# Cross-attention projections in wide token-stationary blocks, some of them with seven products

## The chip, the cores and the metric

The kernel runs on one core of one Trainium2 chip. The metric is the time on the device in microseconds (us), the median of several executions. The core has five engines that this text speaks of: PE (TensorE, matrix products), DVE (VectorE), ACT (ScalarE), POOL (GpSimd, nearly idle here) and SP (SyncE, which only issues the transfers). Each takes its own instructions in a fixed order; between engines they wait for each other by semaphores.

## What is computed

One layer of an encoder on 256 tokens of 2048 channels, all in f32: a half-step SwiGLU FFN, a mixer (pooling and gated linear attention), a cross-attention to 256 memory tokens, a second FFN, and a last RMSNorm. The change touches the cross-attention alone:

```python
def mem_cross_attention(h, mem_h, w_q, w_kv, w_o):
    q = (h @ w_q).reshape(b, s, XATTN_HEADS, XATTN_HEAD_DIM)          # 4 heads of 512
    kv = (mem_h @ w_kv).reshape(b, mem_h.shape[1], 2, XATTN_HEADS, XATTN_HEAD_DIM)
    k, v = kv[:, :, 0], kv[:, :, 1]
    logits = jnp.einsum('bshd,bmhd->bhsm', q, k).astype(jnp.float32) * (XATTN_HEAD_DIM ** -0.5)
    p = jax.nn.softmax(logits, axis=-1).astype(v.dtype)
    o = jnp.einsum('bhsm,bmhd->bshd', p, v).reshape(b, s, D_MODEL)
    return o @ w_o
...
        x = x + mem_cross_attention(rms_norm(x, xattn_norm[l]), rms_norm(mem, mem_norm[l]),
                                    xattn_w_q[l], xattn_w_kv[l], xattn_w_o[l])
```

h and mem_h have 256 rows and 2048 columns; w_q is 2048 x 2048 and w_kv 2048 x 4096.

## The kernel before

**Numbers in two parts.** PE multiplies fp32r values, which hold fewer bits than f32. Each operand is therefore split into a high part (ACT copies it to fp32r) and a low part (DVE subtracts the high part from the source). A product is made of three: high x high, high x low, low x high. Weights go through the same split on their way: a transfer brings 1 MB into `raw`, ACT writes `wh`, DVE writes `wl` (lines 261 and 262).

**Units.** All weights are read as units of 1 MB, numbered through the program; unit 182 is the first of w_q, 198 the first of w_kv, 230 the first of w_o. The class `Stream` emits them: a unit's split is emitted two units ahead of its products (AHEAD = 2), three `raw` buffers are on their way (RAW = 3), and `wh` and `wl` have three buffers, so the split of unit u waits until PE is done with unit u - 3. Other work is put in with `st.op(f, n)`: it is emitted after n further units. The framework then orders each engine's instructions, so what is emitted late can stand earlier or later on an engine.

**Three block forms.** `block_a` (line 307) is feature-stationary: weights are the stationary operand, 512 columns at a time, and the result has features in rows. Per 128 rows of weight and 128 columns it takes one product with a moving operand of 512 (both parts of the activations) and one of 256; a unit has 32 products. `block_t` and `block_b` are token-stationary: a tile of 128 tokens is the stationary operand, and 512 columns of weights stream; a unit has 24 products, and tokens are in rows. `block_s` (line 469) is token-stationary with 1024 columns at a time, so a unit is two chunks of 128 rows x 1024 columns (a pair). Some of its pairs, the sevens, replace the eight block products of a 2 x 2 scheme by seven (as Strassen and Winograd do): 21 products instead of 24. For these, sums of the activations are made once (`Sums.make`, tile `ye`), and per unit sums of the weights in a tile `T` (line 442), which are split like weights (`split_seven`: `xh`, `xl` for three of the raw quarters, `wh`, `wl` for T). PSUM has four tiles of [128, 2, 512]. A `block_s` with sevens holds all four: two for the whole results and two for parts; `combine` adds the parts up after the last seven and frees two, `join` adds them to the whole after the last unit.

**The cross-attention before.** Four `block_a` for the queries, one head each, so q comes out with features in rows, as the logits want it; `ev_Q` joins the halves and multiplies by the row factor R of the norm, which `spread_norm` had spread over the partitions. Then, head by head: `block_a` for the keys, `logits`, `probs`, `block_b` for the values, `values`. The activations of both come from the same tile `xs`: `fold` (line 727) transposes x into it (tiles `px`, 16 per half of x), and `mem_fold` (line 1201, tiles `tm`) later puts the memory tokens in its place. Both write high parts on ACT (line 230) and low parts on DVE (line 231). `mem_fold(c)` writes chunks 4c to 4c + 3, and was emitted after units 2, 3, 4 and 5 of the last head's stretch, one group at a time between units.

The lines that the steps touch:

```python
    for h in range(H):
        if h == H - 1:
            for c in range(4):
                st.op(lambda c=c: mem_fold(c), c + 2)
        block_a(wblock(w_q, h * NB), xs, ev_Q(h))
```

## Time and profile before

| | |
|---|---|
| median of 3 runs | 2093.89 us (2093.42 to 2094.82) |
| profiled execution | 2093.61 us |
| its span | 2091.2 us |
| PE busy | 2079.7 us, 99% |
| DVE busy | 1729.1 us, 83% |
| ACT busy | 1115.5 us, 53% |
| granted TensorE clock | 0.998 |

The profiled execution's own time is 2.4 us above its span, which runs from the first to the last instruction; it is 0.3 us below the median. Busy time is the union of an engine's instructions, but matmuls overlap in their pipeline: a single one is shown with about 390 ns where the next starts about 227 ns later. What a stretch of products costs is therefore read from starts or from the chain, not from the mean of one.

### The profile page before, as it was taken

Reading aid. Unit: us, or ns where it says so; the run is one execution under the profiler, and the core shown is the slowest. Engines: PE = TensorE matmul, PEld = TensorE weight load, DVE = VectorE, ACT = ScalarE, POOL = GpSimd, SP = SyncE. Lnnn points to the kernel's source line nnn. Section 1 sums busy time; section 2 is a strip of 40 time slices with the busy share of each in tenths; the row PEclk is TensorE's granted clock in tenths of the full one; section 3 lists DMA queues with packets and bytes.
Section 4 is the critical chain, followed back from the end, with each engine's and each line's share of the span. In section 5 each row is a group of like instructions: output and inputs, shape, how many; then the busy total and the mean of one; then the engine's idle time right before and its main releaser. Section 6 shows DMA issues by size and latency. Waiting matters only on the chain.

```text
span 2091.2 us, 24553 instructions
## 1 busy us (share of the span) xinstructions
PE 2079.7 (99%) x9901; PEld 1741.6 (83%) x9901; DVE 1729.1 (83%) x1568; ACT 1115.5 (53%) x1096; POOL 14.2 (1%) x41
## 2 busy tenths in 40 slices
PE   9999999999999999999999999999999999999998
PEld 7888888888888888888888888888888888888886
DVE  7999899989998677688665555879998999989974
ACT  7655455645554555365645444556554556545544
POOL 0000000000000000000000000000000000000001
PEclk9999999999999999999999999999999999999999
DMA  7656666567656655468655555656576765676673
GB/s 263 203 200 231 231 221 218 185 224 245 216 199 241 215 179 195 151 193 269 233 181 170 170 165 167 228 190 220 181 241 211 244 203 187 223 241 221 207 257 119
DMA packets 143608, 435.94 MB, mean 208 GB/s; under 512 B 9860, under 2 KB 13544, under 8 KB 143112
## 3 DMA queue, kind: packets, MB, share of 16 engines
q1 hardware_dynamic: 143464, 434.38, 62.7%
q8 instruction: 77, 1.26, 0.2%
q14 instruction: 35, 0.29, 0.0%
q10 hardware_dynamic: 32, 0.01, 0.0%
HBM read 417.58 MB, written 16.78 MB: 208 GB/s over the span
## 4 chain that ended last, share of the span: by engine, by line
PE 96%; DVE 2%; issue 1%; ACT 0%; DMA 0%; SPq 0%; DVEq 0%
PE pt L344 45%; PE pt L465 22%; PE pa L329 15%; PE pb L344 6%; PE pe L344 3%; PE ph L821 1%; PE pl L1247 1%; PE pv L1284 1%; PE px L733 1%; DVE wl L446 0%; DVE T L442 0%; DVE wl L262 0%; DVE xl L262 0%; PE pp L958 0%; DMA x<-in_x 0%
## 5 line engine op out<-in xcount | busy, mean ns | idle before, releaser
L262 DVE TENSOR_TENSOR wl<-raw,wh 128x2048 fp32r<-128x2048 f32 (+2 forms) x279 | 626.4, 2250 | 231.3 <-ACT wh L261 230.3
L261 ACT CAST wh<-raw 128x2048 fp32r<-128x2048 f32 (+2 forms) x279 | 523.2, 1880 | 336.4 <-PE pt L344 106.6
L344 PE MATMUL pt<-wh,xs 128*128 128x512 f32 x1536 | 495.0, 390 | 0.2 <-ACT xs L230 0.2
L344 PE MATMUL pt<-wh,ys 128*128 128x512 f32 x1360 | 427.7, 390 | 0.0
L445 ACT CAST wh<-T 128x1024 fp32r<-128x1024 f32 x206 | 217.0, 1054 | 347.0 <-DVE T L442 336.4
L344 PEld LDWEIGHTS pt<-wh,xs 128*128 128x128 f32 x1536 | 287.6, 188 | 59.3 <-ACT xs L230 0.4
L329 PE MATMUL pa<-xs,wh 128*128 128x512 f32 x896 | 316.0, 397 | 0.0
L344 PE MATMUL pt<-wl,xs 128*128 128x512 f32 x768 | 299.8, 390 | 0.0
L344 PEld LDWEIGHTS pt<-wh,ys 128*128 128x128 f32 x1360 | 254.9, 188 | 52.6
L344 PE MATMUL pt<-wl,ys 128*128 128x512 f32 x680 | 264.9, 390 | 0.0
L329 PE MATMUL pa<-xs,wl 128*128 128x256 f32 x896 | 248.4, 281 | 0.0
L446 DVE TENSOR_TENSOR wl<-T,wh 128x2048 fp32r<-128x2048 f32 x103 | 235.3, 2284 | 1.3 <-ACT wh L445 1.3
L329 PEld LDWEIGHTS pa<-xs,wh 128*128 128x128 f32 x896 | 167.6, 188 | 38.1 <-issue 0.3
L262 DVE TENSOR_TENSOR xl<-raw,xh 128x1536 fp32r<-128x1536 f32 x103 | 180.4, 1751 | 0.0
L329 PEld LDWEIGHTS pa<-xs,wl 128*128 128x128 f32 x896 | 169.1, 189 | 1.7 <-issue 0.2
L344 PEld LDWEIGHTS pt<-wl,xs 128*128 128x128 f32 x768 | 144.2, 188 | 30.0 <-DVE wl L262 0.2
L261 ACT CAST xh<-raw 128x1536 fp32r<-128x1536 f32 x103 | 152.4, 1479 | 13.4 <-DMA raw<-in_ffn_w_gate 8.7
L344 PEld LDWEIGHTS pt<-wl,ys 128*128 128x128 f32 x680 | 127.7, 188 | 26.3
L442 DVE TENSOR_TENSOR T<-T,raw 128x512 f32<-128x512 f32 x206 | 142.3, 691 | 5.7
L442 DVE TENSOR_TENSOR T<-raw 128x1024 f32<-128x1024 f32 x103 | 125.5, 1219 | 0.5
L465 PE MATMUL pt<-wh,xs 128*128 128x512 f32 x320 | 124.5, 389 | 0.0
L465 PE MATMUL pt<-wh,xe 128*128 128x512 f32 x320 | 124.5, 389 | 0.0
(236 smaller groups left out, 2412.1 us busy)
## 6 DMA issues: line engine op xcount, KB each, us to landing
raw<-in_ffn_w_down SPq DMA_DIRECT2D x88, 1024.0 KB, 5.6
raw<-in_ffn_w_up SPq DMA_DIRECT2D x80, 1024.0 KB, 5.1
raw<-in_ffn_w_gate SPq DMA_DIRECT2D x77, 1024.0 KB, 5.1
raw<-in_w_in SPq DMA_DIRECT2D x32, 1024.0 KB, 5.2
raw<-in_xattn_w_kv SPq DMA_DIRECT2D x32, 1024.0 KB, 5.4
raw<-in_w_out SPq DMA_DIRECT2D x16, 1024.0 KB, 5.6
raw<-in_xattn_w_q SPq DMA_DIRECT2D x16, 1024.0 KB, 5.5
raw<-in_xattn_w_o SPq DMA_DIRECT2D x16, 1024.0 KB, 5.7
```

The costliest lines, as they stand in the source:

```text
L261: in_turn("scalar", lambda: nc.scalar.copy(hi, src))
L262: in_turn("vector", lambda: nc.vector.tensor_tensor(out=lo, in0=src, in1=f32(hi), op=ALU.subtract))
L329: nc.tensor.matmul(o, w, x, start=k == 0 and i == 0, stop=last and i == 1)
L344: nc.tensor.matmul(ps, a, w, start=first and i == 0, stop=last and i == 2)
L442: in_turn("vector", lambda: nc.vector.tensor_tensor(out=o, in0=a, in1=b, op=ALU.add))
L445: in_turn("scalar", lambda: nc.scalar.copy(th[:, c], t[:, c]))
L446: in_turn("vector", lambda: nc.vector.tensor_tensor(out=tl, in0=t, in1=f32(th), op=ALU.subtract))
L465: nc.tensor.matmul(banks[n], x, w, start=n in fresh and j == 0, stop=n in ends and j == 2)
L733: nc.tensor.transpose(v[:, j, h * P : (h + 1) * P], x[:, h, j * P : (j + 1) * P], ident)
L821: nc.tensor.transpose(v[:, i, h * P : (h + 1) * P], g[:, h, i * P : (i + 1) * P], ident)
L1247: nc.tensor.matmul(ps[:, t, :M], ys[:, 4 * h + d, a, tok], xa["K"][:, d, b, :], start=i == 0, stop=i == 11,)
L1284: nc.tensor.matmul(ps[:, d, :S], xa["V"][:, m, a, col], xa["PT"][:, m, b, :], start=i == 0, stop=i == 5,)
```

## The change

Queries, keys and values are now made by `block_s`, two heads (1024 columns) at a time: two blocks for w_q with pairs 1, 2 and 3 as sevens, two for the keys and two for the values with pairs 0 and 2 as sevens. That makes 6 + 4 + 4 = 14 sevens among 48 units. The order in which a block takes its pairs is written out (`Q_ORDER`, `KV_ORDER`). Q and K now come with tokens in rows; `rows_turned` transposes them, 8 transposes of 128 x 128 for each head (`turn_Q`, `turn_K`). The row factor of Q is a per-row scale on ACT, and R is no longer spread. Logits, softmax and values keep their work, for two heads one after the other. `mem_fold` is emitted after units 7, 7, 8 and 8 counted from the end of the first query block. The weight sums `T` use the buffers of `sg` (x rows and block results), and `xh`, `xl` share two buffers `att`; which tiles share is switched between the stretches (`homes`).

```diff
 
+    def rows_turned(g):
+
+        v = four(ptile(uid("ph")))
+        for i in range(4):
+            for h in range(2):
+                nc.tensor.transpose(
+                    v[:, i, h * P : (h + 1) * P], g[:, h, i * P : (i + 1) * P], ident
+                )
+        return v
...
-    st.op(open_scope("s_x", {
-        "T": [("kv", D, 2)], "xh": [("kv", D, 2), ("att", 3 * NB, 3)], "xl": [("att", 3 * NB, 3)],
-        "t": [("att", 3 * NB, 3)], "P": [("att", 3 * NB, 3)],
-        "PT": [("att", 3 * NB, 3)],
-    }), 1)
+
+    OUT_HOMES = {"T": [("kv", D, 2)], "xh": [("kv", D, 2), ("att", 3 * NB, 2)],
+                 "xl": [("att", 3 * NB, 2), ("PT", D, 1)]}
+    Q_HOMES = {"T": [("sg", D, 2)], "xh": [("att", 3 * NB, 2)],
+               "xl": [("PT", D, 1), ("att", 3 * NB, 2)]}
+    KV_HOMES = {"T": [("sg", D, 2)], "xh": [("att", 3 * NB, 2)], "xl": [("att", 3 * NB, 2)]}
+
+    def homes(of):
+        return lambda: scope.update(shared={tag: list(of[tag]) for tag in of})
+
+    st.op(open_scope("s_x"), 1)
+    st.op(homes(OUT_HOMES), 1)
...
-    into_x(I["w_out"][0], ys, 1.0, G_X)
+    into_x(I["w_out"][0], ys, 1.0, G_X, spread_too=False)
+    st.op(homes(Q_HOMES))
     st.op(mem_in, 2)
...
-    def ev_Q(h):
-        def evict(p, ps):
-            t = ttile()
-            joined(ps, t, rows["R"])
-            split_pair(ys, 4 * h + 2 * p, t)
+
+    q_sums, Q_ORDER = Sums("ye", xs, (1, 2, 3), True, 2), ((0, 6, 1, 4, 2, 5, 3, 7),
+                                                           (0, 4, 1, 5, 2, 6, 3, 7))
+    kv_sums, KV_ORDER = Sums("ye", xs, (0, 2), True, 2), (1, 3, 4, 0, 5, 6, 2, 7)
+    held = {}
+
+    def ev_Q(b):
+        def evict(j, c):
+            for h in range(2):
+                nc.scalar.activation(c[:, h, :], c[:, h, :], AF.Copy, scale=Rcol[:, h : h + 1])
+            held["Q", b, j] = c
         return evict
 
-    def ev_K(p, ps):
-        if p == 0:
-            xt("K", [P, 4, 2, M], F32R, tag="kv", bufs=2)
-        t = ttile()
-        joined(ps, t)
-        split_pair(xa["K"], 2 * p, t)
-
-    def ev_V(ps):
-        V = xt("V", [P, 2, 2, XHD], F32R, tag="kv", bufs=2)
-        split(V[:, :, 0, :], V[:, :, 1, :], ps)
+    def turn_Q(b, j):
+        k = 8 * b + 4 * j
+        split(ys[:, k : k + 4, 0, :], ys[:, k : k + 4, 1, :], rows_turned(held["Q", b, j]))
+
+    def turn_K(h):
+        v = rows_turned(held["K", h])
+        K = xa["K", h] = xt("K", [P, 4, 2, M], F32R, tag="kv", bufs=2)
+        split(K[:, :, 0, :], K[:, :, 1, :], v)
+
+    def ev_V(b):
+        def evict(j, c):
+            V = xa["V", 2 * b + j] = xt("V", [P, 2, 2, XHD], F32R, tag="kv", bufs=2)
+            split(V[:, :, 0, :], V[:, :, 1, :], c)
+        return evict
...
-        nm, sm = xt("nm", [P, 2]), xt("sm", [P, 2])
+        nm, sm = xt("nm", [P, 2], bufs=2), xt("sm", [P, 2], bufs=2)
...
-        pr = xa["P"] = shared_tile("P", 2 * M, F32, uid("P"), 1).rearrange("p (t m) -> p t m", t=2)
+        pr = xa["P", h] = xt("P", [P, 2, M], bufs=2)
...
-        PT = xa["PT"] = shared_tile("PT", 4 * S, F32R, uid("PT"), 1).rearrange(
+        if h % 2 == 0:
+            xt("PT", [P, D], F32R)
+        PT = xa["PT", h] = xa["PT"][:, h % 2 * 4 * S : (h % 2 + 1) * 4 * S].rearrange(
             "p (m a s) -> p m a s", m=2, a=2
         )
...
-    for h in range(H):
-        if h == H - 1:
-            for c in range(4):
-                st.op(lambda c=c: mem_fold(c), c + 2)
-        block_a(wblock(w_q, h * NB), xs, ev_Q(h))
-    for h in range(H):
-        block_a(wblock(w_kv, h * NB), xs, ev_K)
-        st.op(lambda h=h: logits(h), 2)
-        st.op(lambda h=h: probs(h), 3)
-        block_b(wblock(w_kv, D + h * NB), xs, ev_V)
-        st.op(lambda h=h: values(h), 1)
+    for g, after in zip(q_sums.pairs, (0, 1, 3)):
+        st.op(lambda g=g: among_weights(lambda: q_sums.make(g)), after)
+    for b in range(2):
+        block_s(wwide(w_q, b * 2 * NB), xs, q_sums, Q_ORDER[b], ev_Q(b))
+        for j in (1, 0):
+            st.op(lambda b=b, j=j: turn_Q(b, j), 1)
+        if b == 0:
+            for c, after in enumerate((7, 7, 8, 8)):
+                st.op(lambda c=c: mem_fold(c), after)
+    st.op(homes(KV_HOMES))
+    for g, after in zip(kv_sums.pairs, (1, 2)):
+        st.op(lambda g=g: among_weights(lambda: kv_sums.make(g)), after)
+    for b in range(2):
+        block_s(wwide(w_kv, b * 2 * NB), xs, kv_sums, KV_ORDER, lambda j, c, b=b: held.__setitem__(
+            ("K", 2 * b + j), c))
+        for j in (1, 0):
+            h = 2 * b + j
+            st.op(lambda h=h: turn_K(h), 1)
+        for h in (2 * b, 2 * b + 1):
+            st.op(lambda h=h: logits(h), 2)
+            st.op(lambda h=h: probs(h), 3)
+        block_s(wwide(w_kv, D + b * 2 * NB), xs, kv_sums, KV_ORDER, ev_V(b))
+        for h in (2 * b, 2 * b + 1):
+            st.op(lambda h=h: values(h), 1)
+    st.op(homes(OUT_HOMES))
     OUTPUT.make_sums()
     into_x(w_o, ys, 1.0, G_FFN2, spread_too=False)
     st.op(close_scope, 1)
```

How it moves instructions is shown at two places.

The first place is the start of the queries, on DVE. Tiles: `x267` holds the second half of x, and the two lines that write it from `pt259` and `pt260` add the last results of w_out; `px` are its transposes, of which the low parts go to `xs`; `wl184` belongs to the third unit of w_q. Before:

```order
L710 SCALAR_TENSOR_TENSOR x267_7136<-pt259_7038,x267_7136 128x2x512
L710 SCALAR_TENSOR_TENSOR x267_7136<-pt260_7039,x267_7136 128x2x512
L262 TENSOR_TENSOR wl184_7336<-raw184_7245,wh184_7335 128x2048
L283 TENSOR_REDUCE sums_101<-ss_100 128x2
L206 TENSOR_SCALAR chain_102<-sums_101 128x2
L210 RECIPROCAL Rcol_98<-chain_102 128x2
L216 TENSOR_TENSOR chain_102<-chain_102,Rcol_98 128x2
L217 TENSOR_TENSOR chain_102<-chain_102 128x2
L218 RECIPROCAL Rcol_98<-chain_102 128x2
L222 TENSOR_SCALAR diag279_7462<-ident_73,Rcol_98 128x128
L231 SCALAR_TENSOR_TENSOR xs_107<-px273_7375,gains_97,xs_107 128x256
```

Now, from just before the second of these additions on:

```order
L413 TENSOR_TENSOR j272_7336<-j272_7336 128x128
L713 SCALAR_TENSOR_TENSOR x267_7136<-pt260_7039,x267_7136 128x2x512
L414 TENSOR_TENSOR j272_7336<-j272_7336 128x128
L268 TENSOR_TENSOR xs_107<-j272_7336,xs_107 128x128
L415 SCALAR_TENSOR_TENSOR j272_7336<-j272_7336 128x128
L418 TENSOR_TENSOR j272_7336<-j272_7336 128x128
L445 TENSOR_TENSOR T184_7346<-raw184_7245 128x1024
L268 TENSOR_TENSOR ye271_7335<-j272_7336,ye271_7335 128x384
L445 TENSOR_TENSOR T184_7346<-T184_7346,raw184_7245 128x512 x2
L262 TENSOR_TENSOR xl184_7350<-raw184_7245,xh184_7349 128x1536
L449 TENSOR_TENSOR wl184_7348<-T184_7346,wh184_7347 128x2048
L231 SCALAR_TENSOR_TENSOR xs_107<-px275_7387,gains_97,xs_107 128x256
```

Unit 184 was a plain unit of one DVE instruction; it is a seven now, and its sums and both its low parts, with the sums of the activations (`j272`, `ye271`), stand ahead of the first write of `xs` from `px`. The unit after the first one is also another: it was the one with chunks 4 to 7, and it is pair 6 (chunks 12 and 13), which comes from the last of the two `px` tiles.

The second place is the change from queries to keys, where `xs` gets the memory tokens. On DVE, before (`tm319` to `tm321` are the transposes of the memory tokens, `wl198` and `wl199` the first two units of w_kv, `t322` a part of the queries of the last head):

```order
L262 TENSOR_TENSOR wl198_8038<-raw198_7894,wh198_8037 128x2048
L231 SCALAR_TENSOR_TENSOR xs_107<-tm319_8020,gains_97,xs_107 128x256 x3
L262 TENSOR_TENSOR wl199_8093<-raw199_7939,wh199_8092 128x2048
L231 SCALAR_TENSOR_TENSOR xs_107<-tm319_8020,gains_97,xs_107 128x256
L231 SCALAR_TENSOR_TENSOR xs_107<-tm320_8075,gains_97,xs_107 128x256 x2
L301 TENSOR_TENSOR t322_8147<-pa315_7941,c323_8148 128x512
L305 TENSOR_TENSOR t322_8147<-t322_8147,R284_7511 128x512
L262 TENSOR_TENSOR wl200_8155<-raw200_7986,wh200_8154 128x2048
```

Now (`sg313` is the result of the second query block, `tm311`, `tm312`, `tm314` and `tm315` the four groups):

```order
L545 TENSOR_TENSOR sg313_8022<-pt305_7749,sg313_8022 128x1024
L545 TENSOR_TENSOR sg313_8022<-pt306_7750,sg313_8022 128x1024
L262 TENSOR_TENSOR wl200_8098<-raw200_7935,wh200_8097 128x2048
L231 SCALAR_TENSOR_TENSOR xs_107<-tm311_7988,gains_97,xs_107 128x256
L231 SCALAR_TENSOR_TENSOR xs_107<-tm312_8005,gains_97,xs_107 128x256
L231 SCALAR_TENSOR_TENSOR xs_107<-tm314_8057,gains_97,xs_107 128x256
L231 SCALAR_TENSOR_TENSOR xs_107<-tm315_8074,gains_97,xs_107 128x256
L231 SCALAR_TENSOR_TENSOR xs_107<-tm311_7988,gains_97,xs_107 128x256
L231 SCALAR_TENSOR_TENSOR xs_107<-tm312_8005,gains_97,xs_107 128x256
L406 TENSOR_TENSOR j321_8152<-xs_107 128x512
```

The groups had stood one after the other between units; they now stand together behind the two joins and the split of unit 200, the third of w_kv, and take turns.

On ACT the high parts of the same tiles, before:

```order
L261 CAST wh198_8037<-raw198_7894 128x2048
L230 ACTIVATE xs_107<-tm319_8020,gains_97 128x256 x3
L261 CAST wh199_8092<-raw199_7939 128x2048
L230 ACTIVATE xs_107<-tm319_8020,gains_97 128x256
L230 ACTIVATE xs_107<-tm320_8075,gains_97 128x256 x2
L300 COPY c323_8148<-pa315_7941 128x512
L261 CAST wh200_8154<-raw200_7986 128x2048
L300 COPY c328_8212<-pa316_7942 128x512
```

and now:

```order
L261 CAST wh199_8027<-raw199_7908 128x2048
L261 CAST wh200_8097<-raw200_7935 128x2048
L230 ACTIVATE xs_107<-tm311_7988,gains_97 128x256
L261 CAST xh201_8165<-raw201_7965 128x1536
L230 ACTIVATE xs_107<-tm312_8005,gains_97 128x256
L1248 ACTIVATE sg313_8022<-sg313_8022,Rcol_98 128x512 x2
L230 ACTIVATE xs_107<-tm314_8057,gains_97 128x256
L1248 ACTIVATE sg313_8022<-sg313_8022,Rcol_98 128x512 x2
L230 ACTIVATE xs_107<-tm315_8074,gains_97 128x256
L230 ACTIVATE xs_107<-tm311_7988,gains_97 128x256
L230 ACTIVATE xs_107<-tm312_8005,gains_97 128x256
```

Among the first of them now stand a weight cast of unit 201 and four scalings of the query rows. On PE all 32 transposes of the memory tokens follow the last product of the queries, with no unit between them, and take all four PSUM tiles; behind them stands unit 198, whose result needs one of these tiles back.

## The prediction

> **What bounds the kernel now.** I read the page's first lines and its chain first, then PE's waits:

> ```profile
> span 2091.2 us, 24553 instructions
> ...
> PE 2079.7 (99%) x9901; PEld 1741.6 (83%) x9901; DVE 1729.1 (83%) x1568; ACT 1115.5 (53%) x1096; POOL 14.2 (1%) x41
> ...
> PE 96%; DVE 2%; issue 1%; ACT 0%; DMA 0%; SPq 0%; DVEq 0%
> ```

> ```profile
> PE pwarm L200 <- POOL ident masks.py:199: 1.4, 1, 1.4
> PE px L669 <- DMA x<-in_x: 0.2, 1, 0.2
> PE pt L344 <- ACT xs L230: 0.2, 1, 0.2
> ```

> The rows are busy us by engine, then the chain's shares, then all waits of PE (total, times, longest). PE is the chain, and after its start it waits for nothing worth 0.2 us. So a product saved is time saved, and a wait added to PE is time lost; what the other engines do counts only where PE comes to wait for it. The stretches of the chain give PE's rates (start, us, what):

> ```profile
> 132.61 0.87 PE ph L821 x8
> ...
> 158.70 7.25 PE pt L465 x32
> ...
> 811.10 27.23 PE pb L344 x120
> ...
> 1004.80 1.75 PE px L733 x16
> ...
> 1017.85 0.44 PE ps L227 x4
> ...
> 1018.29 61.64 PE pa L329 x352
> ```

> A `block_a` unit of 32 products costs 61.64/352 x 32 = 5.60 us. A token-stationary unit of 24 costs 27.23/120 x 24 = 5.45 us, a seven of 21 costs 7.25/32 x 21 = 4.76 us. Eight transposes cost 0.87 us.

> **The change, part by part: PE's work.** Before: 32 `block_a` units for Q and K (179.3 us) and 16 `block_b` units for V (87.1 us), 266.4 us. Now 34 plain units (185.2 us) and 14 sevens (66.6 us), 251.8 us: **-14.6 us**. Added: 8 groups of transposes for Q and K, all on PE's path: 8 x 0.87 = **+7.0 us**. Removed: the spreading of R, **-0.4 us**. Logits, probabilities, values and the 32 transposes of the memory keep their number. So PE's own work falls by 8.0 us; the question is what PE will wait for.

> **DVE.** A seven costs DVE much more than a plain unit. Rows of the groups (us in all, mean ns of one):

> ```profile
> L262 DVE TENSOR_TENSOR wl<-raw,wh 128x2048 fp32r<-128x2048 f32 (+2 forms) x279 | 626.4, 2250 | 231.3 <-ACT wh L261 230.3
> ...
> L446 DVE TENSOR_TENSOR wl<-T,wh 128x2048 fp32r<-128x2048 f32 x103 | 235.3, 2284 | 1.3 <-ACT wh L445 1.3
> ...
> L262 DVE TENSOR_TENSOR xl<-raw,xh 128x1536 fp32r<-128x1536 f32 x103 | 180.4, 1751 | 0.0
> ...
> L442 DVE TENSOR_TENSOR T<-T,raw 128x512 f32<-128x512 f32 x206 | 142.3, 691 | 5.7
> ...
> L442 DVE TENSOR_TENSOR T<-raw 128x1024 f32<-128x1024 f32 x103 | 125.5, 1219 | 0.5
> ...
> L542 DVE TENSOR_TENSOR sg<-pt,sg 128x1024 f32<-128x1024 f32 x40 | 47.3, 1217 | 0.3
> ...
> L231 DVE SCALAR_TENSOR_TENSOR xs<-px,gains,xs 128x256 fp32r<-128x256 f32 x64 | 29.4, 481 | 11.6 <-ACT xs L230 11.3
> ...
> L410 DVE TENSOR_TENSOR j<-j 128x128 f32<-128x128 f32 x21 | 6.1, 289 | 0.5
> ...
> L268 DVE TENSOR_TENSOR xe<-j,xe 128x384 fp32r<-128x384 f32 x8 | 4.4, 552 | 0.0
> ```

> A seven takes 1.22 + 2 x 0.69 + 1.75 + 2.28 = 6.63 us of DVE against 4.76 us of PE; a plain unit takes 2.25 against 5.45. In the query stretch, 6 x 6.63 + 10 x 2.25 = 62 us, and by the same rows (0.69 us for 512 columns, 1.22 for 1024) two combinations and one pair of joins come to 7.7 us, one pair of splits of Q to 2.4, three sums of activations to 3 x 2.7, eight writes of `xs` to 3.9, and the scaling of the memory rows to 2 x 1.3: 25 us more. That makes 87 us of DVE beside 83.1 + 3.5 us of PE. That is as full as the FFN, where PE still never waits:

> ```profile
> 1459.50:1541.10 81.60, 81.60 (x369) 67.47 (x368) 80.88 (x64) 46.98 (x39) 0.00 (x0) 1.00 0.59 197
> ```

> (stretch, its length, then busy us of PE, PE's loads, DVE, ACT and POOL.) PE 81.60 and DVE 80.88 of 81.60. I cost the DVE work inside the blocks at nothing, covered by the splits being two units ahead; if that cover is gone, it is a rival below. Keys and values have only 4 sevens in 16 units and more slack.

> **The first handover, w_out to the queries.** Rows of the timeline (start, us, what, and the wait before it). On DVE:

> ```profile
> 999.67 1.22 DVE L710 SCALAR_TENSOR_TENSOR x<-pt,x 128x1024 f32<-128x1024 f32 x1 [0.52 <-PE pt L344]
> ...
> 1007.00 0.48 DVE L231 SCALAR_TENSOR_TENSOR xs<-px,gains,xs 128x256 fp32r<-128x256 f32 x1
> ...
> 1009.05 0.48 DVE L231 SCALAR_TENSOR_TENSOR xs<-px,gains,xs 128x256 fp32r<-128x256 f32 x1 [0.54 <-ACT xs L230]
> 1010.08 0.88 DVE L231 SCALAR_TENSOR_TENSOR xs<-px,gains,xs 128x256 fp32r<-128x256 f32 x2 [0.54 <-ACT xs L230]
> ...
> 1013.55 0.48 DVE L231 SCALAR_TENSOR_TENSOR xs<-px,gains,xs 128x256 fp32r<-128x256 f32 x1 [0.54 <-ACT xs L230]
> ```

> and on ACT:

> ```profile
> 1004.48 1.28 ACT L209 ACT_TABLE_LOAD   x1
> ```

> Eight writes of `xs` run from 1007.0 to 1014.0, and each pair of high and low part takes 1.03 us, since ACT and DVE wait for each other. Before, PE went on after the transposes with chunks 4 to 7, long ready, and needed chunks 8 to 15 only 5.6 and 11.2 us later. Now the next unit is chunks 12 and 13, the fifth and sixth of these writes, and the order on DVE puts unit 184's seven ahead: four small sums and a split at 0.29 us, 0.55 for `ye`, and 6.63, less 0.08 us at each of ten seams, where the next starts before the last ends: about 8 us after the addition that ends at 1000.9, so the first write begins at 1008.9, not 1007.0. The table load and the root of the norm, which ran ahead of the writes before, stand between the first and the third now and cost about 1 us more. The high part of chunk 12 thus comes at about 1008.9 + 3 x 1.03 + 1 + 0.2 = 1013.2. PE is through its transposes at about 1006.1 (its first unit is 0.15 us shorter, two products earlier). Idle: **+7.1 us**. Bounds: 4.2 us, if the writes keep their old times (the fifth was ready at 1010.4), and 9 us, if PE needs both parts of both chunks.

> **The second handover, queries to keys.** Let E be the end of the last query product. The order puts all 32 transposes of the memory behind E. They need PSUM that the joins free, and unit 198 needs a tile back whose four chunks are all written. On ACT stand, up to the last write of the first group: the cast of unit 200 (whose buffer PE frees at E), that of three quarters of unit 201, four scalings of the query rows, and 13 of the 16 high parts:

> ```profile
> L261 ACT CAST wh<-raw 128x2048 fp32r<-128x2048 f32 (+2 forms) x279 | 523.2, 1880 | 336.4 <-PE pt L344 106.6 <-PE pa L329 65.3 <-issue 64.5
> ...
> L261 ACT CAST xh<-raw 128x1536 fp32r<-128x1536 f32 x103 | 152.4, 1479 | 13.4 <-DMA raw<-in_ffn_w_gate 8.7
> ...
> L803 ACT ACTIVATE sg<-sg,Rcol 128x512 f32<-128x512 f32 x36 | 23.2, 714 | 15.9 <-DVE sg L542 15.9
> ...
> L230 ACT ACTIVATE xs<-tm,gains 128x256 fp32r<-128x256 f32 x16 | 7.3, 472 | 11.3 <-DVE xs L231 9.8 <-PE tm L1206 1.4
> ```

> 1.88 + 1.48 + 4 x 0.71 + 13 x 0.47 = 12.3 us, and 0.8 us for the DVE write behind it and a small sum: E + 13, some tenths less for the seams. DVE's own queue (the joins, unit 200's low part, at E + 4.4) is through before. PE has 4 x 0.87 = 3.5 us of transposes in that time. Idle: **+9.4 us**. Bounds: 1.5 us, if one group's four writes run alone as before (4 x 1.03 us from E + 0.9), and 14.9 us, if all 16 pairs run at 1.03 us behind the cast (1.9 + 16.5 - 3.5). I take the sum of the queue, since ACT takes its instructions in order.

> **The clock after a pause.** This is the row that speaks most against an idle PE. The granted clock is the figure behind POOL's:

> ```profile
> 2083.00:2084.00 1.00, 0.00 (x0) 0.00 (x0) 0.53 (x5) 0.71 (x4) 0.00 (x0) 0.99 0.39 143
> 2084.00:2085.00 1.00, 0.00 (x0) 0.00 (x0) 0.93 (x3) 0.47 (x1) 0.00 (x0) 0.50 1.00 348
> ```

> PE's first instructions and its last, from the timeline:

> ```profile
> 1.42 2.82 PE L200 MATMUL pwarm<-ident 128*128 128x128 f32 x12 [1.42 <-POOL ident masks.py:199]
> ...
> 5.28 0.60 PE L200 MATMUL pwarm<-ident 128*128 128x128 f32 x4
> ```

> ```profile
> 2081.24 0.39 PE L344 MATMUL pe<-wh,ys 128*128 128x512 f32 x1
> ```

> 2.4 us after the last product the clock stands at 0.50. Both pauses above are longer. How long it takes to rise again is to be seen only at the start: twelve transposes of 128 x 128 take 2.82 us, about 0.22 us each, twice the 0.87/8 = 0.11 us of later ones, and four at 5.28 take 0.60 us, again 0.11 us each behind the first. So half speed lasts 3 to 4 us and costs half of that: **+1.7 us** for each pause, +3.4 us. Bounds: 0 and 3.5 us for each. [...]

> **What else moves.** The transfers stay 48 of 1 MB, 1024 columns wide. The fetch of x for w_o, which had been issued during the queries, moves on SP to w_o's third unit, since its buffer serves `T` now; it is read first after five units of w_o, 27 us later: nothing. The second seven's `T` waits for the store of x; its turn on DVE comes behind the eight writes of `xs`, over 12 us after the addition that the store waits for: nothing. For the softmax of a head these rows bear, the last from the chain:

> ```profile
> 1183.00 0.69 DVE L1253 TENSOR_REDUCE nm<-pl 128x2 f32<-128x512 f32 x1
> ...
> 1185.24 0.62 DVE L1263 TENSOR_SCALAR P<-P,sm 128x256 f32<-128x256 f32 x2
> ```

> ```profile
> 1229.41 2.87 PE pl L1247 x24
> ```

> From 1183.0 to 1185.9 it takes 2.9 us, with a table load 4.2 us. Behind the first head's logits PE now has the second head's (2.87 us) and 19 products of 0.227 us, 7.2 us in all, before it wants the probabilities: nothing.

> **Sum.** -14.6 + 7.0 - 0.4 + 7.1 + 9.4 + 3.4 = **+11.9 us** on the profiled 2093.6 us: 2105.5 us, and 2105.8 us for the median, which stands 0.3 us higher. What a measurement of this kernel can tell from no change is about 0.2%, 4.2 us. With the pauses' own bounds the likeliest case lies from 2100 to 2112 us.

> **The rivals.**
> - *Only the second handover stops PE: 2097 us.* The first is hidden if ACT and DVE come to chunk 12 while PE still has filler: six products of unit 184 stand behind the first four of unit 183 and need older chunks. Against it: they stand behind, and PE takes them in order. 2105.8 - 7.1 - 1.7 = 2097.0, within 0.2%.
> - *Faster, both handovers hidden: 2086 us.* The mechanism is the one chain of high and low parts: if a group's writes follow each other without the foreign casts, the first group is done at E + 5 and the first pause is short too. It decides once the two pauses and their clock together stay below 4 us. The 1.03 us per pair speaks against it. 2093.9 - 8.0 = 2085.9.
> - *Sevens held up by their buffers: 2115 us.* `xh` and `xl` share two buffers in Q and V, so a seven's cast can wait for the last product of the seven before; then 1.48 + 1.75 = 3.2 us stand open, at three places in Q and V: +9.6. For it speaks that the order lets units overtake there; against it, that a plain unit of 5.45 us lies between.
> - *The clock, either way.* If it holds through both pauses, 2105.8 - 3.4 = 2102 us; against it stands the fall to 0.50 at the end. If it takes the upper bound of 3.5 us to make up for each pause, 2105.8 + 3.6 = 2109 us; against it stands the start, where half speed lasts 3 to 4 us and not 7. [...]

> **How the numbers follow.** Both pauses as summed 0.46, with the clock holding 0.10, with the slower clock 0.08, buffers on top 0.13: slower, 0.77. Only the second handover 0.12: within 0.2%. Both hidden 0.11: faster. The forecast is the likeliest case, 2105.8 us. From 2095 to 2115 us lie nearly all of the first three, most of the case with the second handover alone and about half of the buffers' case, some 0.8; what is left out is the faster case and the upper half of the buffers'.

> **What would show it.** PE's waits should hold two new rows, of about 7 us for `xs` at the start of the queries and of about 9 us at the first product of the keys, and granted clock at 0.5 in both; elsewhere PE stays at 100%. PE's busy time should fall by about 5 us (8.0 less what the slow clock adds), and the stretch from the first product of Q to the first of w_o grow by 12 us. Wrong would be: DVE late inside the query blocks, a pause behind the softmax, or a PE whose chain shows no wait in either place.

## The result, and the profile after

The changed kernel takes 2106.87 us (median of 6 runs, 2105.16 to 2107.32), the kernel before, on the same chip, 2094.12 us (2093.42 to 2095.16). The ratio is 1.0059, with a 95% interval from 1.0046 to 1.0071: 0.6% slower, 12.8 us. The profiled execution of the changed kernel took 2107.17 us. The first lines of its page and its chain:

```profile
span 2105.4 us, 24203 instructions
...
PE 2076.7 (99%) x9663; PEld 1730.7 (82%) x9663; DVE 1806.6 (86%) x1654; ACT 1137.8 (54%) x1124; POOL 14.1 (1%) x41
...
PE 95%; DVE 3%; ACT 1%; issue 1%; DMA 0%; SPq 0%; DVEq 0%
```

All waits of PE in the changed kernel (total us, times, longest):

```profile
PE pt L344 <- DVE xs L231: 9.0, 1, 9.0
PE pt L344 <- ACT xs L230: 6.9, 1, 6.9
PE pwarm L200 <- POOL ident masks.py:199: 1.4, 1, 1.4
PE px L672 <- DMA x<-in_x: 1.3, 1, 1.3
PE pt L468 <- DVE xl L262: 0.2, 1, 0.2
```

Two rows are new, and each is one single wait. The spans differ by 14.2 us: PE is busy 3.0 us less (2079.7 to 2076.7), the two new waits are 15.9 us, and the wait for the first transfer of x, at the start of the program, was 1.1 us longer in this execution than in the one profiled before (in the runs below, which start with the same code, it lies between nothing and 2.0 us). That makes 14.0 us.

The next fence has windows of the changed kernel, laid over the two pauses and the first products behind each (stretch, length, then busy us of PE, PE's loads, DVE, ACT, POOL; the granted clock is the figure behind POOL's):

```profile
1007.40:1014.30 6.90, 0.03 (x1) 0.00 (x0) 4.98 (x12) 5.16 (x12) 0.00 (x0) 0.85 0.47 152
1014.30:1018.80 4.50, 4.46 (x11) 3.50 (x12) 2.84 (x7) 2.83 (x4) 0.00 (x0) 0.50 0.00 0
1100.60:1109.60 9.00, 0.02 (x1) 0.05 (x1) 7.40 (x19) 8.61 (x21) 0.00 (x0) 0.71 0.45 155
1109.60:1114.40 4.80, 4.80 (x11) 3.77 (x12) 4.76 (x11) 0.52 (x1) 0.00 (x0) 0.50 0.00 0
```

What PE waited for in the first pause is told by the chain of the changed kernel (start, us, what):

```profile
1006.75 0.94 ACT wh L448
...
1007.72 2.29 DVE wl L449
1010.01 0.41 DVE xs L231
...
1010.44 0.47 ACT xs L230
...
1010.93 1.28 ACT L209
...
1013.02 0.41 DVE xs L231
...
1013.45 0.85 ACT xs L230 x2
...
1014.34 2.08 PE pt L344 x4
```

The low part of unit 184's seven (L449) ends at 1010.0, then come the first write of `xs`, the table load (L209) and the writes up to the high part of chunk 12. In the second pause ACT has no gap up to the 13th high part; its timeline:

```profile
1097.13 1.92 ACT L261 CAST wh<-raw 128x2048 fp32r<-128x2048 f32 x1 [3.27 <-PE pt L344]
1098.95 0.46 ACT L230 ACTIVATE xs<-tm,gains 128x256 fp32r<-128x256 f32 x1
1099.37 1.48 ACT L261 CAST xh<-raw 128x1536 fp32r<-128x1536 f32 x1
1100.76 0.47 ACT L230 ACTIVATE xs<-tm,gains 128x256 fp32r<-128x256 f32 x1
1101.12 1.32 ACT L1248 ACTIVATE sg<-sg,Rcol 128x512 f32<-128x512 f32 x2
1102.35 0.46 ACT L230 ACTIVATE xs<-tm,gains 128x256 fp32r<-128x256 f32 x1
1102.70 1.32 ACT L1248 ACTIVATE sg<-sg,Rcol 128x512 f32<-128x512 f32 x2
1103.93 4.05 ACT L230 ACTIVATE xs<-tm,gains 128x256 fp32r<-128x256 f32 x10
```

Two casts, four scalings and 13 high parts stand in a row, up to 1108.0 us. PE starts at 1109.58, 1.6 us after them and behind DVE's low part. The chain of the changed kernel shows what the last 5 us hung on:

```profile
1104.42 1.27 DVE xs L231 x3
1105.69 0.60 DVE j L406
1106.29 1.18 DVE xs L231 x3
1107.47 0.20 DVE j L413
1107.66 1.18 DVE xs L231 x3
1108.85 0.20 DVE j L414
1109.04 0.41 DVE xs L231
...
1109.58 0.77 PE pt L344
```

ACT sets the pace up to 1104.4. From there DVE has ten low parts and three steps of the sums of activations (L406, L413, L414) to do without a gap before the tile that PE waits for is through.

### The profile page after: what moved, and what is told of

Read it like the earlier page. It is cut to its first block, busy times and chain, and to the rows that moved or that the text cites. A ratio compares the mean times of both kernels' runs of the same rounds, so it can differ in the third digit from the quotient of the medians.

```text
span 2105.4 us, 24203 instructions
## 1 busy us (share of the span) xinstructions
PE 2076.7 (99%) x9663; PEld 1730.7 (82%) x9663; DVE 1806.6 (86%) x1654; ACT 1137.8 (54%) x1124; POOL 14.1 (1%) x41
## 4 chain that ended last, share of the span: by engine, by line
PE 95%; DVE 3%; ACT 1%; issue 1%; DMA 0%; SPq 0%; DVEq 0%
PE pt L344 53%; PE pt L468 25%; PE pa L329 6%; PE pe L344 3%; PE pb L344 2%; PE ph L735 1%; DVE wl L449 1%; PE pl L1273 1%; PE pv L1312 1%; DVE T L445 1%; PE px L746 0%; DVE xl L262 0%; DVE wl L262 0%; DMA x<-in_x 0%; PE pp L966 0%
## 5 line engine op out<-in xcount | busy, mean ns | idle before, releaser
L262 DVE TENSOR_TENSOR wl<-raw,wh 128x2048 fp32r<-128x2048 f32 (+2 forms) x265 | 593.9, 2247 | 154.0 <-ACT wh L261 153.1
L344 PE MATMUL pt<-wh,xs 128*128 128x512 f32 x2080 | 670.5, 391 | 16.0 <-DVE xs L231 9.0
L261 ACT CAST wh<-raw 128x2048 fp32r<-128x2048 f32 (+2 forms) x265 | 496.7, 1879 | 295.3 <-PE pt L344 132.3
L344 PEld LDWEIGHTS pt<-wh,xs 128*128 128x128 f32 x2080 | 391.0, 189 | 97.3 <-issue 9.2
L344 PE MATMUL pt<-wh,ys 128*128 128x512 f32 x1360 | 428.0, 390 | 0.0
L344 PE MATMUL pt<-wl,xs 128*128 128x512 f32 x1040 | 407.3, 392 | 0.0
L344 PEld LDWEIGHTS pt<-wh,ys 128*128 128x128 f32 x1360 | 254.8, 188 | 52.7
L449 DVE TENSOR_TENSOR wl<-T,wh 128x2048 fp32r<-128x2048 f32 x117 | 267.3, 2285 | 6.3 <-ACT wh L448 5.5
L344 PE MATMUL pt<-wl,ys 128*128 128x512 f32 x680 | 264.9, 390 | 0.0
L344 PEld LDWEIGHTS pt<-wl,xs 128*128 128x128 f32 x1040 | 196.1, 189 | 40.6
L262 DVE TENSOR_TENSOR xl<-raw,xh 128x1536 fp32r<-128x1536 f32 x117 | 204.9, 1752 | 19.8 <-ACT xh L261 18.6
L261 ACT CAST xh<-raw 128x1536 fp32r<-128x1536 f32 x117 | 173.1, 1479 | 43.6 <-PE pt L468 31.6
L445 DVE TENSOR_TENSOR T<-T,raw 128x512 f32<-128x512 f32 x234 | 161.5, 690 | 6.3
L344 PEld LDWEIGHTS pt<-wl,ys 128*128 128x128 f32 x680 | 127.7, 188 | 26.2
L468 PE MATMUL pt<-wh,xs 128*128 128x512 f32 x376 | 146.4, 389 | 0.0
L445 DVE TENSOR_TENSOR T<-raw 128x1024 f32<-128x1024 f32 x117 | 142.6, 1219 | 0.5
L468 PE MATMUL pt<-xh,xs 128*128 128x512 f32 x376 | 141.4, 392 | 0.1
L329 PE MATMUL pa<-xs,wh 128*128 128x512 f32 x384 | 135.0, 396 | 0.0
L329 PE MATMUL pa<-xs,wl 128*128 128x256 f32 x384 | 106.6, 281 | 0.0
L329 PEld LDWEIGHTS pa<-xs,wh 128*128 128x128 f32 x384 | 71.7, 188 | 16.0 <-issue 0.3
```

The costliest lines, as they stand in the source:

```text
L261: in_turn("scalar", lambda: nc.scalar.copy(hi, src))
L262: in_turn("vector", lambda: nc.vector.tensor_tensor(out=lo, in0=src, in1=f32(hi), op=ALU.subtract))
L329: nc.tensor.matmul(o, w, x, start=k == 0 and i == 0, stop=last and i == 1)
L344: nc.tensor.matmul(ps, a, w, start=first and i == 0, stop=last and i == 2)
L445: in_turn("vector", lambda: nc.vector.tensor_tensor(out=o, in0=a, in1=b, op=ALU.add))
L449: in_turn("vector", lambda: nc.vector.tensor_tensor(out=tl, in0=t, in1=f32(th), op=ALU.subtract))
```

## The experiments

The theory: of the 12.8 us, two single places are the cause, each with its idle time and the slow products behind it; without them the change is a gain. The rival: DVE is so full in the queries that the pauses only show a lack that would come out elsewhere. The runs of the kernel before that stand beside the experiments took 2093.5 to 2094.1 us, so a difference between two experiments is good to some 0.5 us.

**The first block in another order.** Its second unit takes old chunks; the sevens had to change with it (pair 6 for pair 1), so that it is a plain unit.

```diff
-    q_sums, Q_ORDER = Sums("ye", xs, (1, 2, 3), True, 2), ((0, 6, 1, 4, 2, 5, 3, 7),
-                                                           (0, 4, 1, 5, 2, 6, 3, 7))
+    q_sums, Q_ORDER = Sums("ye", xs, (2, 3, 6), True, 2), ((0, 1, 2, 4, 3, 5, 6, 7),
+                                                           (0, 4, 2, 5, 3, 1, 6, 7))
```

> The first block of the queries takes its chunks in another order (pairs 0, 1, 2, 4, 3, 5, 6, 7, with sevens 2, 3 and 6), so that its first three units read chunks that were written long before; the second block has the same sevens. Theory of the two pauses: the first pause of the changed kernel (6.9 us without a product, and ten products at 0.43 us in place of 0.227 us behind it, 2.2 us) goes and nothing else moves: 2106.9 - 9.1 = 2097.8 us, with the second pause as it was (9 us). Rival, DVE full: DVE has 87 us of work beside the 86.6 us of PE in the queries, and the pause was time that it needed; the wait comes back at later units of the block: 2104 to 2107 us, with PE waits for DVE inside the query blocks.

Measured: 2102.53 us (4 runs; before 2093.72 us; ratio 1.0042, 1.0027 to 1.0057). Half of the expected gain, 4.3 us of 9.1. The waits of PE in the queries and keys:

```profile
PE pt L344 <- DVE xs L231: 8.9, 1, 8.9
PE pt L468 <- DVE xs L231: 1.8, 1, 1.8
PE pt L344 <- DVE wl L262: 1.6, 2, 1.0
...
PE pt L468 <- ACT xh L261: 0.5, 1, 0.5
```

The pause of 6.9 us is gone, and with it the fall of the clock (1.00 from 1004 to 1024 us), but 1.8 + 1.6 + 0.5 = 3.9 us came back in short waits, 3.3 us of them between 1015 and 1024 us. Both theories are partly right: the chunk made the pause, and behind it DVE was late anyway.

**The second block in another order, and the memory's groups earlier.**

```diff
-                                                           (0, 4, 1, 5, 2, 6, 3, 7))
+                                                           (0, 1, 4, 2, 3, 5, 6, 7))
-            for c, after in enumerate((7, 7, 8, 8)):
+            for c, after in enumerate((5, 6, 7, 8)):
```

> The second block of the queries takes its pairs as 0, 1, 4, 2, 3, 5, 6, 7 (sevens 1, 2, 3 as before), so that the four groups of the memory can be turned after its units 5, 6, 7 and 8 and not all at its end; the first block is as in the changed kernel. Theory of the two pauses: the second pause (9.0 us without a product, 2.3 us of slow products) goes, the first stays at 6.9 us: 2106.9 - 11.3 = 2095.6 us. Rival, ACT and DVE full: three sevens in four units and the 16 pairs of writes among them come late elsewhere, and the first units of the keys or the last ones of the queries wait instead: 2101 to 2107 us.

Measured: 2096.82 us (10 runs; ratio 1.0015, 1.0006 to 1.0024), 10.1 us less than the changed kernel. The wait of 9.0 us is gone, the 6.9 us at the first handover are as before, and the waits for a seven's low part grew from 0.2 to 1.4 us. The theory held here. What lets the groups go early is that the third seven is the fifth unit now: the PSUM tiles of the sevens' parts come free with three units of the queries left, and PE turns the first group at 1090.4 us, 10.6 us ahead of the last two.

**Both orders.** The first experiment's kernel with pairs 0, 1, 2, 4, 3, 6, 5, 7 in the second block.

```diff
-                                                           (0, 4, 2, 5, 3, 1, 6, 7))
+                                                           (0, 1, 2, 4, 3, 6, 5, 7))
-            for c, after in enumerate((7, 7, 8, 8)):
+            for c, after in enumerate((6, 6, 7, 8)):
```

> Both orders together: the query blocks take their pairs as 0, 1, 2, 4, 3, 5, 6, 7 and 0, 1, 2, 4, 3, 6, 5, 7 with sevens 2, 3 and 6, and the groups of the memory are turned after units 6, 6, 7 and 8 of the second. Theory of the two pauses: 2106.9 - 9.1 - 11.3 = 2086.5 us, 0.36% faster than the kernel before, since only the 8.0 us less work of PE is left of the change; no PE wait over 1 us. Rival, DVE full: the pauses were time that DVE and ACT needed, and without them at least half of it comes back as waits inside the blocks: 2095 us or more.

Measured: 2100.28 us (6 runs; ratio 1.0031, 1.0020 to 1.0043). The expected 2086.5 us were missed by 14 us. The short waits of the first block are the same as in the first experiment. And a part of the second pause is back. The third seven is the sixth unit here and not the fifth, and the groups are emitted later by up to one unit: PE turns the first of them at 1090.6 us, 5.2 us ahead of the third, where the second experiment had 10.6 us. PE's timeline at the last two groups and the first product of the keys:

```profile
1095.80 1.04 PE L1221 MATMUL tm<-ident,mem 128*128 128x128 f32 x8
1097.28 1.09 PE L1221 MATMUL tm<-ident,mem 128*128 128x128 f32 x8 [0.44 <-DVE sg L545]
1103.20 0.80 PE L344 MATMUL pt<-wh,xs 128*128 128x512 f32 x1 [4.82 <-DVE xs L231]
```

A lead of one unit less goes with a pause of 4.8 us and its slow clock; in the second experiment and in the runs below with the first seven behind the writes, with 18 and with 6 sevens and with pair 4, all with groups emitted after units 5, 6, 7 and 8, the lead is 10.6 us or more and the keys start without a wait. The place of the seven and that of the groups were changed together, so no run tells which of the two decides.

**More work for PE in the pauses.**

```diff
-        for j in range(4):
-            for h in range(2):
-                nc.tensor.transpose(
-                    v[:, j, h * P : (h + 1) * P], x[:, h, j * P : (j + 1) * P], ident
-                )
+        for i in range(6 if c == 3 and gain == G_X else 1):
+            for j in range(4):
+                for h in range(2):
+                    nc.tensor.transpose(
+                        v[:, j, h * P : (h + 1) * P], x[:, h, j * P : (j + 1) * P], ident
+                    )
...
+        for i in range(6 if c == 3 else 1):
...
```

(The second loop stands around the transposes of `mem_fold` in the same way.)

> The changed kernel with more work for PE: the eight transposes of the last group of x, and those of the last group of the memory, are done six times over with the same result, so that PE works for 4.4 us more in each pause and no wait for its inputs moves. If the slow products come of the pause (the granted clock falls to 0.5 when PE rests 4 to 5 us and rises 5 us after it resumes): the clock stays at 1.0 over both pauses, the waits shrink to 2.5 and 4.6 us, and the kernel is faster with more work: 2106.9 - 2.2 - 2.3 = 2102.4 us. If the products are slow for another reason: 2106.9 us. If the repeated transposes hold up the writes behind them, since these wait for the last one: up to 4.4 us more for each pause, 2107 to 2116 us.

Measured: 2103.91 us (4 runs; 2103.82 to 2105.23; ratio 1.0051, 1.0034 to 1.0068), about 3.0 us faster than the changed kernel, with 80 transposes more. At the first pause PE waited 2.5 us, the clock stayed at 1.00, and the windows from 1015 to 1024 us show six or seven products in each us, where the slow ones show three or four: 2.2 us gained. At the second PE still waited 3.6 us, and the clock fell all the same, for 6.83 us. That pause itself, the extra transposes included, was 1 us shorter. By the two chains, DVE has 8 low parts and two steps of the sums between ACT's last piece (1101.6 us here) and PE's start, where the changed kernel has 10 and three: the last group's transposes end later, so its writes stand less far ahead, and two low parts and one step are 1.0 us. So at the first pause the slow products do come of PE's rest, and the fall can be avoided with work that is of no use; at the second the rest was not filled enough to show it.

**The first seven behind the writes.** Now the first three units are all plain, and the third seven of the second block is its fifth unit.

```diff
-    q_sums, Q_ORDER = Sums("ye", xs, (1, 2, 3), True, 2), ((0, 6, 1, 4, 2, 5, 3, 7),
-                                                           (0, 4, 1, 5, 2, 6, 3, 7))
+    q_sums, Q_ORDER = Sums("ye", xs, (2, 3, 6), True, 2), ((0, 1, 4, 2, 5, 3, 6, 7),
+                                                           (0, 2, 1, 3, 6, 4, 5, 7))
-            for c, after in enumerate((7, 7, 8, 8)):
+            for c, after in enumerate((5, 6, 7, 8)):
```

> Sevens 2, 3 and 6; the first query block takes its pairs as 0, 1, 4, 2, 5, 3, 6, 7, so that its first three units are plain and the first seven's 6.6 us of DVE stand behind the eight writes of xs and not ahead of them; the second takes 0, 2, 1, 3, 6, 4, 5, 7, with the sevens as its second, fourth and fifth unit as in the second experiment, and the memory's groups after units 5, 6, 7, 8. Theory now: the pauses are a matter of what stands in DVE's and ACT's queues ahead of the writes at the handover, not of their total. Both pauses go, with at most 2 us of short waits left and no fall of the clock: 2106.9 - 6.9 - 9.0 - 4.5 = 2086.5 us, up to 2088.5 us. Rival, DVE's total: the 87 us of DVE beside 86.6 us of PE leave no room, and the 4 us of waits inside the first block that the first experiment showed come back in any order: 2091 to 2095 us.

Measured: 2097.29 us (10 runs; ratio 1.0018, 1.0009 to 1.0027), 9 us above the upper end of the theory's range and 2 us above the rival's. The keys start without a wait. In the first block PE waits 2.3 us for the high part of the first seven and 1.8 us for its low part, and the clock falls again, for 6.83 us. DVE's timeline shows why:

```profile
1016.90 0.48 DVE L231 SCALAR_TENSOR_TENSOR xs<-px,gains,xs 128x256 fp32r<-128x256 f32 x1 [0.54 <-ACT xs L230]
1017.30 0.68 DVE L406 TENSOR_TENSOR j<-xs 128x512 f32<-128x512 f32 x1
...
1019.42 1.22 DVE L445 TENSOR_TENSOR T<-raw 128x1024 f32<-128x1024 f32 x1
...
1022.35 1.75 DVE L262 TENSOR_TENSOR xl<-raw,xh 128x1536 fp32r<-128x1536 f32 x1
1024.02 2.29 DVE L449 TENSOR_TENSOR wl<-T,wh 128x2048 fp32r<-128x2048 f32 x1
```

The eight writes last until 1017.4, the sums of activations until 1019.4, and the seven's own 6.6 us until 1026.3; PE has done what it can of the seven at 1019.5 and waits. Fourth in the block is one plain unit too early.

**More sevens, fewer sevens.** From that kernel, a third seven in each block of keys and values,

```diff
-    kv_sums, KV_ORDER = Sums("ye", xs, (0, 2), True, 2), (1, 3, 4, 0, 5, 6, 2, 7)
+    kv_sums, KV_ORDER = Sums("ye", xs, (0, 2, 5), True, 2), (1, 3, 0, 4, 2, 6, 5, 7)
-    for g, after in zip(kv_sums.pairs, (1, 2)):
+    for g, after in zip(kv_sums.pairs, (1, 2, 3)):
```

> The kernel of the run before, with three sevens in place of two in each of the four blocks of keys and values (pairs 0, 2 and 5, order 1, 3, 0, 4, 2, 6, 5, 7). A seven is 0.69 us shorter than a plain unit: if only PE's work counts there, 2.8 us less than the run before, about 2084 us. Rival, DVE full as in the queries: 6 x 6.63 + 10 x 2.25 = 62 us in two blocks with the joins, splits and softmax beside 89 us of PE is no more than in the queries, but the casts and splits of values, logits and probabilities come in bursts: waits eat the gain, no faster than the run before.

and, again from that kernel, one seven in each block of queries, keys and values:

```diff
-    q_sums, Q_ORDER = Sums("ye", xs, (2, 3, 6), True, 2), ((0, 1, 4, 2, 5, 3, 6, 7),
+    q_sums, Q_ORDER = Sums("ye", xs, (2,), True, 2), ((0, 1, 4, 2, 5, 3, 6, 7),
-    kv_sums, KV_ORDER = Sums("ye", xs, (0, 2), True, 2), (1, 3, 4, 0, 5, 6, 2, 7)
+    kv_sums, KV_ORDER = Sums("ye", xs, (2,), True, 2), (1, 3, 4, 0, 5, 6, 2, 7)
```

> The kernel of the first run of these four with 6 sevens in place of 14 (one pair in each block, pair 2), the orders as there for the queries and as in the changed kernel for keys and values. If a seven is worth 0.69 us of PE each, as summed in the prediction: 8 x 0.69 = 5.5 us more than the first run, 2092 us where that stands at 2086.5 us. Rival, the sevens cost as much in DVE's delays as they save in PE: the same time as the first run within 1 us.

Measured: 2104.63 us with 18 sevens (4 runs; ratio 1.0053, 1.0038 to 1.0068), 2097.29 us with 14, and 2092.60 us with 6 (10 runs; ratio 0.9996, 0.9987 to 1.0006). The theory that counts PE's work alone is wrong in both, even in sign: among these three kernels a seven more costs time. The rival of the second, the same time within 1 us, is wrong too. The clock has a part in it: it fell for 6.83 us in the first query block with 18 and with 14 sevens, and with 6 it was 1.00 from 1000 to 1300 us. With 18, PE waits for DVE and ACT in the keys and values too; rows of its waits in the whole run, of which the second belongs to the first query block and is there with 14 as well:

```profile
PE pt L468 <- DVE xl L262: 5.3, 8, 1.6
PE pt L468 <- ACT wh L448: 2.3, 1, 2.3
PE pt L344 <- DVE wl L262: 1.5, 1, 1.5
...
PE pt L468 <- ACT xh L261: 1.3, 2, 0.6
```

PE's waits in the queries, keys and values come to 12.4 us with 18 sevens (17 waits), 6.7 us with 14 (6 waits) and 1.7 us with 6 (2 waits).

**Pair 4 in the second unit.** The second experiment's kernel, with only the second unit's chunks changed at the first handover (pairs 4, 5 and 6 change places in the first block); the seven stays ahead of the writes.

```diff
-    q_sums, Q_ORDER = Sums("ye", xs, (1, 2, 3), True, 2), ((0, 6, 1, 4, 2, 5, 3, 7),
+    q_sums, Q_ORDER = Sums("ye", xs, (1, 2, 3), True, 2), ((0, 4, 1, 5, 2, 6, 3, 7),
```

> The second experiment's kernel, with one more edit: the first query block takes pair 4 as its second unit (order 0, 4, 1, 5, 2, 6, 3, 7) in place of pair 6; the seven stays third and its DVE work ahead of the writes. Chunks 8 and 9 are the first two of the eight writes, 12 and 13 the fifth and sixth. By the changed kernel's own trace chunk 8's parts are there at 1008.1 and 1010.4 us and chunk 9's at 1010.9 and 1011.4 us, so that PE, at 1007.4 us, waits some 3 us in pieces and not 6.9 us, and too short for the clock to fall: 2096.8 - 3.9 - 2.2 = 2090.7 us. If the seven's place is what counts and the chunk is not: the pause stays near 6 us, 2095 us or more.

Measured: 2094.33 us (10 runs; ratio 1.0004, 0.9994 to 1.0014), 2.5 us less than the second experiment and 3.6 us more than expected. The pause of 6.9 us became waits of 0.7 and 1.2 us, with the queues of DVE and ACT in the same order as before, so the chunk decided it. What was off: the clock fell even so, for 3.4 us, and 3.0 us of short waits stand further on in the queries. Of these the second experiment had 1.4 us already; the other 1.6 us, in the rest of the first block and at the transposes of its result, are new.

**Two sevens or one in the queries, the first of them fifth.**

```diff
-    q_sums, Q_ORDER = Sums("ye", xs, (1, 2, 3), True, 2), ((0, 6, 1, 4, 2, 5, 3, 7),
-                                                           (0, 4, 1, 5, 2, 6, 3, 7))
+    q_sums, Q_ORDER = Sums("ye", xs, (2, 3), True, 2), ((0, 1, 4, 5, 2, 6, 3, 7),
+                                                           (0, 1, 2, 4, 3, 5, 6, 7))
-    for g, after in zip(q_sums.pairs, (0, 1, 3)):
+    for g, after in zip(q_sums.pairs, (2, 4)):
-            for c, after in enumerate((7, 7, 8, 8)):
+            for c, after in enumerate((5, 6, 7, 8)):
```

> Queries with two sevens in place of three in each block (pairs 2 and 3, their sums of activations made after units 2 and 4), the first block in the order 0, 1, 4, 5, 2, 6, 3, 7, so that the first seven comes fifth, behind all eight writes of xs and two plain units; the second in the order 0, 1, 2, 4, 3, 5, 6, 7, the memory's groups after units 5, 6, 7 and 8; keys and values as in the changed kernel, whose blocks showed no wait. Theory: DVE keeps up in the queries (4 x 6.63 + 12 x 2.25 = 54 us and 25 us of other work beside 84.5 us of PE) and nothing stands ahead of the writes, so that of the change only PE's work is left: 7.5 us less than the kernel before by the accounting of the runs, less 2 x 0.69 us: 6.1 us less, 2093.9 - 6.1 = 2087.8 us, 0.3% faster than before. Rival: wherever the sevens stand in the queries, their 6.6 us of DVE against 4.8 us of PE comes late to a wait of 2 to 4 us: 2090 to 2093 us.

The other kernel differs from this one only in its sums, `(2,)` for `(2, 3)`:

> The same with a single seven in each query block (pair 2, fifth in the first block and third in the second). Two plain units more: 2 x 0.69 = 1.4 us more of PE, 2089.2 us, if the run with two sevens has no waits for DVE in the queries; below that run, if two sevens still wait for DVE.

Measured: 2088.18 us with two sevens (8 runs, 2087.69 to 2089.25; before 2093.51 us; ratio 0.9974, 0.9963 to 0.9984), 2088.47 us with one (8 runs; ratio 0.9975, 0.9965 to 0.9985). Both are faster than the kernel before, by 0.26% and 0.25%, and 18 us faster than the changed kernel. With two sevens the theory held (2087.8 us) and the rival's 2090 us and more did not come; with one, 2088.5 us lie 0.7 us below what was expected without any wait. The page and all waits of PE with two sevens:

```profile
span 2086.3 us, 24183 instructions
...
PE 2073.8 (99%) x9669; PEld 1729.6 (83%) x9669; DVE 1795.9 (86%) x1639; ACT 1134.9 (54%) x1118; POOL 14.2 (1%) x41
```

```profile
PE pwarm L200 <- POOL ident masks.py:199: 1.4, 1, 1.4
PE pt L468 <- DVE xl L262: 1.3, 2, 0.8
```

Neither handover shows a wait, and the granted clock is 1.00 in the windows from 1014 to 1290 us; over the whole span it is 0.998, as in the kernel before. With one seven only 0.5 us of such waits are left, which is most of why it is as fast with two plain units more.

This limits what the kernels with 18, 14 and 6 sevens show. The one with 6 has one seven in each query block and one in each block of keys and values; the last kernel here has one in each query block, later in its place, and two in the others. Each measured against its own runs of the kernel before, the one with 6 gains 1.3 us and the last 5.0 us. Of these 3.7 us, by the rows, four plain units made sevens are 2.8 us, and waits that are gone are 1.2 us. In no kernel with two sevens in these blocks does PE wait inside the keys and values, so there the sevens paid.

## Why the prediction was right

The forecast was 2105.8 us and slower; the measurement is 2106.9 us, with the mechanism as forecast. By its steps:

- **PE's own work, -8.0 us.** Right, as the two last runs show: 2088.18 - 2093.51 = -5.3 us is -8.0 + 1.4 (two sevens fewer) + 1.3 (waits). With the waits and slow products of the changed kernel the same sum is -8.0 + 15.9 + 0.2 + 4.5 + 1.1 = 13.7 us against 14.2 us of span. Transposes and sevens were priced rightly by the rows of before.
- **First handover, +7.1 us.** Measured 6.9 us. The queue was as described: the first write of DVE began at 1009.9 (forecast 1008.9), the table load lay between the first and the third, and PE started with the high part of chunk 12 at 1014.3 (forecast 1013.2), but PE came to it 1.3 us later as well, 1.1 us of that from the first transfer of x at the program's start. The pair 4 run shows that it is the choice of chunk that made the pause.
- **Second handover, +9.4 us.** Measured 9.0 us, with ACT's queue as listed, but the sum is right in part by luck. Counted from the end of the queries (E, 1096.9 us), ACT was through with the 13th high part at E + 11.1 us and not 12.3, since each starts before the last ends (ten high parts took 4.05 us and not 4.7). DVE's write came 1.5 us behind it and not 0.8: DVE's queue, taken to be through before, paced the last 5 us. The two errors nearly cancel. The second experiment shows that the pause goes when the groups are turned earlier, in another order of the block, so no lack of engine time made it.
- **The clock, +1.7 us each.** Too small: 2.2 and 2.3 us, inside the stated bounds of 0 to 3.5. Half speed lasted 4.7 and 5.1 us behind the restart and not 3 to 4. The run with more work shows for the first pause that the rest causes it. No run shows the 3.5 us, on which the case with the slower clock stands: the longest stretch at half speed behind one of these two pauses, 6.0 us in the run with more work, is some 2.7 us, an estimate from the 2.2 us in 4.7 us here.
- **DVE inside the blocks, nothing.** Right for this kernel (0.2 us), but the reason given, that splits run two units ahead, was not enough. The pauses seem to have been the cover: where the first, fifth and pair 4 experiments shorten them, waits of 3 to 7 us stand in the query blocks. I counted 87 us of DVE beside 86.6 us of PE and took the FFN, equally full, as proof that this is hidden. The FFN has no eight writes of `xs` that hold DVE to ACT's pace at 1.03 us a pair just before a seven; that this is the difference is read from DVE's timeline in the fifth experiment, and no run tests it alone.
- **Transfers, softmax, the buffers of sevens.** No wait of PE names them in the changed kernel, but for the first transfer of x. The rival of sevens held by shared buffers did not happen.
- **The foreseen signs.** Two rows of 6.9 and 9.0 us, clock at 0.50 in both, and no other new wait over 0.2 us (the one for the first x, 1.1 us longer, was there before). PE's busy time fell by 3.0 us and not by 5, since the slow clock added 4.5 us and not 3.4. The stretch from the last transposes of x to the first product of w_o grew by 10.4 us, not 12, and what follows it by 3.0 us. The values of two heads, 24 products more than before, stand behind w_o's first products now; I had forgotten that they move.

The faster rival was priced at 2086 us with both handovers hidden. It was not reached with 14 sevens in any order tried; the best runs, 2 us above it, have 12 and 10.

## What to carry to other kernels

A change that only saves products must be read at its two ends, where one stretch hands its buffers to the next. List what stands in the queues of the engines that write there, and give PE units whose data is old until those writes are through; here the choice of the second pair in a table of orders decided over a pause of 6.9 us. Where a helper engine is as full as PE over a stretch, cheaper products that load it more can cost time: with the first of them fourth in its block, 18 were slower than 14, and 14 slower than 6 (2104.63, 2097.29 and 2092.60 us; with 14, DVE was busy for 77.85 us and PE for 75.93 us of the 83 us from 1014 to 1097 us); with the first of them fifth and none too many behind it, 12 and 10 were faster than 6 (2088.18 and 2088.47 us). So count them by stretch and place, and not in all. Both pauses here cost more than PE's rest (6.9 us and 2.2 us of slow products, 9.0 us and 2.3 us), so a wait is priced with the slow products behind it.
